# Three features of an input projection finished one pass earlier, and a planner's due times exchanged for fixed classes

## The chip, the cores and the metric

The kernel runs on one core of one Trainium2 chip, as one program. The metric is the device time of an execution in microseconds (us), as the median of several runs. Five engines work side by side, each with an instruction queue that it takes in order: TensorE (PE in the profile) multiplies, VectorE (DVE) and ScalarE (ACT) do elementwise work, GpSimd (POOL) has a few small steps here, and SyncE (SP) issues nearly all DMA transfers. Results of TensorE go to eight banks of a small memory (PSUM), from which VectorE or ScalarE have to clear them before the bank is used again.

## The reference

One encoder layer on x of 2048 tokens by 1024 features, in float32, cut to what matters:

```python
xn = rms_norm(x, mix_norm_g)
aq, ak, av, mq, mk, mv, mo, i, f, ga, gm = split(xn @ w_in)
A = chunk_band_attention(aq, ak, av, rel_bias)       # 8 heads of 64, own chunk of 64 and 8 before
mq, mk = silu(causal_conv(mq, mk))                    # width 4 along the tokens
M = sigmoid(mo) * rms_norm(mlstm_chunkwise(mq, mk, mv, i, f))   # 4 heads of 128
y = sigmoid(ga) * (A @ w_att_proj) + sigmoid(gm) * (M @ w_mlstm_proj)
x = x + y @ w_out
x = x + square(relu(rms_norm(x) @ w_up)) @ w_down
return rms_norm(x, final_norm_g)
```

## The kernel before

**Numbers and products.** Every float32 operand is split into a rounded high part (ScalarE, a cast) and the rest (VectorE, a subtraction), and each matrix product is three matmuls: high by high, high by low, low by high. A weight tile of 128 x 1024 is split by the two instructions at L582 and L584 (`split_now`); there are three slots for split weights (`wsp`) and four for raw ones (`wraw`). The large products use a scheme with seven products of half-sized sums in place of eight products of halves. The operands of the seven are numbered 0 to 6, and the four quarters of a result (a11, a12, a22, a21; the second place is the half of the tokens) come from sums of them: with p0 to p6 for the products and u2 = p0 + p3, they are a11 = p0 + p1, a12 = u2 + p2 + p4, a22 = u2 + p2 + p5 and a21 = u2 + p5 + p6. The sum v = u2 + p2 is used on the way to a22.

**Tokens.** There are four blocks of 512 tokens. The input projection of blocks 0 and 1 runs first ("quads", L712, all seven products of a feature in a row), and that of blocks 2 and 3 follows in `in_far`, at the same time as the attention and the recurrence (the "mixers") of blocks 0 and 1.

**The input projection of blocks 2 and 3.** `in_far` goes over the ten features of IN_ORDER (gm0, gm1, q, mq, vm, ga0, k, mk, ga1, mo) in three passes, since not all split operands fit at once: products (0, 3, 1), then (2, 4), then (5, 6), as BATCHES says. A product (`product`, L743, or L748 for vm) is one weight tile and 24 matmuls in two banks, for vm two weight tiles and 48. Pass one finishes a11 and parks u2 in device memory (`park_u2`). Pass two fetches u2 (`unpark`, L883), adds it to p2 and parks the sum v (`park_v`, L867), and finishes a12 (`finish_far`, L894). Pass three fetches v and u2 and finishes a22 and a21 (also L894). It goes through the features in the groups of PAIRS. What finishing is depends on the feature: for q and k a split and two stores, for the gates a tanh and a store, for mq and mk the convolution (`conv_far`, with L2208 three times and L2212 once for each result).

**Joint products.** Between the groups of pass three stand two joint products (`joint`, L1134, 168 matmuls each), which project the mixers' results of blocks 0 and 1. Their operands are loaded and split by `take_joint`, and their results, gated and added, become y. `take_y_late` loads y's parts k = 0 to 3 and splits them (L1355) into the operands of the output quads, which follow pass three at once (L712 again). For blocks 2 and 3, `project` does the projection inside the first down projection, at places that PROJ fixes.

**What sets the order.** The order of all instructions is written out when the program is built. A planner (`Flow`) runs the kernel's parts as threads against a model of the engines' times, and always takes the step that can start first. Among steps that could start at the same time, TensorE takes the one with the lower class (its spawn number, 0 to 5). On ScalarE, VectorE, GpSimd and SyncE the kernel before takes evictions marked "!" first and then the step with the earliest due time:

```python
if self.due is not None and e in ENGS:
    prio = -1e12 if prio < 0 else self.due.get((th.name, th.steps), 1e12)
key = (start, prio, th.n)
```

The due times come from a dry run of the whole program with empty tiles (`Blank`), whose log `dues` goes through backwards: a step is due when its earliest user has to begin, less its own duration and the latency between engines. In the dry run the classes decide. The framework underneath may still exchange neighbouring instructions within about 6 us on ScalarE and 10 us on VectorE of the planned time, and keeps the order beyond that.

**The start.** `norm_in` scales the first block's x (L1329, L1331) and squares it for the norm (L1338), and `split_first` splits the first weight tile in two halves (L565, L567). In the code the first square waits for both halves.

Of the kernel before, what the change touches and what calls it, by code (L numbers as in the profile page):

```python
# [28 lines left out]
P = 128  # L29
D = 1024  # L30
S = 2048
T = 512
# [22 lines left out]
PAIRS = ((0, 1), (2, 3), (4,), (5, 6), (7, 8), (9,))  # L55
# [7 lines left out]
JOINT = {(2, 2): 0, (2, 4): 1}  # L63
# [11 lines left out]
ENGS = ("act", "dve", "pool", "sp")  # L75
PEDUE = lambda prio: prio == 5
SPM = 0.0
TRIES = 1


class Event:
    def __init__(self):
        self.at = None
        self.by = ()


class Blank:


    def __getattr__(self, name):  # L90
        return self

    def __getitem__(self, at):
        return self

    def __call__(self, *a, **kw):
        return self

    def __iter__(self):
        raise TypeError("a blank has no parts")  # L100

    def tile(self, *a, **kw):
        return Blank()


class Pool:
    def __init__(self, items):
        self.free = [((0.0, "sp"), n, i, ()) for n, i in enumerate(items)]
        self.n = len(items)
# [15 lines left out]
class Thread:  # L125
    def __init__(self, gen, prio, n, at, name, by):
        self.gen, self.prio, self.n, self.at = gen, prio, n, at
        self.req = None
        self.name, self.kids, self.steps, self.by = name, 0, 0, list(by)


class Flow:
# [14 lines left out]
    def __init__(self, due=None):  # L147
        self.due = due
        self.log, self.cur = [], None
# [6 lines left out]
    def spawn(self, gen, prio=2):  # L156
        up = self.cur
        if up is None:
            th = Thread(gen, prio, self.count, self.now, f"{self.count}", ())
        else:  # L160
            th = Thread(gen, prio, self.count, self.now, f"{up.name}.{up.kids}", up.by)
            up.kids += 1
        self.count += 1
        self._step(th, None)

    def set(self, ev):
        ev.at = self.now
        ev.by = tuple(self.cur.by)

    def put(self, pool, *items, late=0.0):  # L170

        for i in items:
            by = tuple((x, y + late) for x, y in self.cur.by) if self.cur else ()
            pool.free.append(((self.now[0] + late, self.now[1]), pool.n, i, by))
# [4 lines left out]
    def _grant(self, th):  # L179
        kind, r = th.req[0], th.req  # L180
        if kind == "wait":
# [3 lines left out]
            th.by += [x for e in r[1] for x in e.by]  # L185
# [14 lines left out]
        th.by += [x for g in got for x in g[3]]  # L200
# [4 lines left out]
    def _step(self, th, value):  # L205
        keep, up = self.now, self.cur
        while True:
            self.now, self.cur = max(self.now, th.at), th
            try:
                th.req = th.gen.send(value)  # L210
            except StopIteration:
                self.now, self.cur = keep, up
                return
            self.cur = up
# [10 lines left out]
    def run(self):  # L225
        while self.ready or self.blocked:
# [15 lines left out]
            for th in self.ready:  # L242
                t, frm = th.at
                for e in th.req[0].split("|"):
# [12 lines left out]
                    if self.due is not None and e in ENGS:  # L257
                        prio = -1e12 if prio < 0 else self.due.get((th.name, th.steps), 1e12)
# [11 lines left out]
            at = th.name, th.steps  # L270
            self.log.append((at, e, start, end, th.prio, {x: y for x, y in sorted(th.by, key=lambda x: x[1])}))
            th.steps += 1
            th.by = [(at, 0.0)]
            th.at = self.now = (end, e)
            self._step(th, e)


def dues(log):
    late, of = {}, {x[0]: x[1:4] for x in log}
    due = {}  # L280
    for at, e, start, end, prio, by in reversed(log):
        end_by = late.get(at, 1e12) - (SPM if e == "sp" else 0.0)
        begin = end_by - (end - start)
        if e == "pe" and PEDUE(prio):
            begin = min(begin, start)
        due[at] = begin
        for x, wait in by.items():
            lat = Flow.LAT[of[x][0]].get(e, 0.0) + wait
            if e == "pe" and prio < 5:
                lat += Flow.FAR  # L290
            late[x] = min(late.get(x, 1e12), begin - lat)
    return due
# [20 lines left out]
class Layer:  # L313
    LATE, LANDED = 4000.0, 10000.0

    def __init__(self, nc, pool, psum, io, due=None):
# [2499 lines left out]
```

## Time and profile before

| what | value |
|---|---|
| time, median of 3 runs | 2733.04 us (2730.65 to 2734.66) |
| profiled execution, its own time | 2726.03 us |
| its span | 2724.2 us |
| granted clock of TensorE | 0.999 |
| instructions | 38141 |
| moved by DMA | 683.01 MB |

The profile is one execution, taken by the hardware profiler. Times are in us unless marked ns; PE is TensorE's matmuls, PEld its weight loads (which overlap the matmuls), and L12 is line 12 of the kernel. A group row gives line, engine, operation, out<-in by the program's tile names, shapes, the number of instructions, and then busy time, mean ns of one, and the idle time ahead of them with what ended it. A waits row names who waited for whom, the sum in us, how many times, and the longest. The chain that ended last follows the program back from its last instruction, at each step to what released it. Ends of matmuls are modelled, so one takes some 390 ns in these rows while the next starts 227 ns later.

### The profile page before, as it was taken

What the parts mean: (1) busy time and instruction counts of PE and PEld (TensorE: products, weight loads), DVE (VectorE), ACT (ScalarE), POOL (GpSimd) and SP (SyncE); (2) the same over time, 40 slices, a digit from 0 to 9 for tenths busy, and PEclk for the clock granted to TensorE, in tenths of its full rate; (3) what the DMA queues carried; (4) which work ended last, traced back from release to release, by engine and by line L of the source; (5) the groups of instructions that cost most, each with busy time, mean ns of one, the idle gap of its engine ahead of it and who ended that gap; (6) DMA issues with size and microseconds to landing.
All of it is one profiled execution on the core that took longest, in us unless ns stands there. A gap on an engine that the chain in (4) does not pass through costs nothing.

```text
span 2724.2 us, 38141 instructions
## 1 busy us (share of the span) xinstructions
PE 2706.6 (99%) x12784; PEld 2253.2 (83%) x12784; DVE 2109.8 (77%) x3750; ACT 1543.0 (57%) x2685; POOL 48.4 (2%) x79
## 2 busy tenths in 40 slices
PE   9999999999999999999999999999999999999998
PEld 8878888888888888888888888888888888888887
DVE  7878876888876899887768888889798665657675
ACT  6555456776753545566556766656345565554443
POOL 0000000000000000000000000000000000000000
PEclk9999999999999999999999999999999999999999
DMA  8777889878768889867768787766864454578863
GB/s 309 276 261 278 292 288 308 264 239 276 265 231 282 292 306 323 278 215 263 267 235 285 246 261 223 238 232 219 277 229 160 163 197 159 189 271 281 275 241 134
DMA packets 339304, 683.01 MB, mean 251 GB/s; under 512 B 37684, under 2 KB 66996, under 8 KB 339108
## 3 DMA queue, kind: packets, MB, share of 16 engines
q1 hardware_dynamic: 338388, 679.52, 73.2%
q8 instruction: 100, 1.64, 0.3%
q10 hardware_dynamic: 720, 1.06, 0.1%
q14 instruction: 96, 0.79, 0.1%
HBM read 461.41 MB, written 215.88 MB: 249 GB/s over the span
## 4 chain that ended last, share of the span: by engine, by line
PE 91%; DVE 3%; DMA 2%; issue 2%; ACT 1%; SPq 0%; POOL 0%; ACTq 0%; POOLq 0%; DVEq 0%
PE bank L712 40%; PE bank L743 9%; PE bank L644 8%; PE bank L645 8%; PE bank L643 8%; PE bank L1134 3%; PE bank L748 2%; PE bank L1612 2%; PE bank L1580 2%; PE bank L1505 2%; PE bank L970 1%; DVE wsp L584 1%; PE bank L1855 0%; PE bank L1840 0%; DMA ctx<-park 0%
## 5 line engine op out<-in xcount | busy, mean ns | idle before, releaser
L712 PE MATMUL bank<-r,wsp 128*128 128x512 f32 x4872 | 1110.3, 389 | 0.8 <-DVE wsp L584 0.7
L712 PEld LDWEIGHTS bank<-r,wsp 128*128 128x128 f32 x4872 | 913.2, 188 | 192.4 <-DVE wsp L584 1.2
L582 ACT CAST wsp<-wraw 128x1024 fp32r<-128x1024 f32 x437 | 459.1, 1051 | 495.3 <-PE bank L712 165.0
L584 DVE TENSOR_TENSOR wsp<-wraw,wsp 128x1024 fp32r<-128x1024 f32 x437 | 533.7, 1221 | 233.6 <-ACT wsp L582 228.6
L643 PE MATMUL bank<-r,wsp 128*128 128x512 f32 x960 | 379.3, 395 | 0.0
L645 PE MATMUL bank<-r,wsp 128*128 128x512 f32 x960 | 375.2, 391 | 0.0
L644 PE MATMUL bank<-r,wsp 128*128 128x512 f32 x960 | 375.2, 391 | 0.0
L743 PE MATMUL bank<-r,wsp 128*128 128x512 f32 x1512 | 368.1, 393 | 1.2 <-DVE ctx L894 1.0
L743 PEld LDWEIGHTS bank<-r,wsp 128*128 128x128 f32 x1512 | 279.0, 188 | 56.8 <-issue 1.0
L645 PEld LDWEIGHTS bank<-r,wsp 128*128 128x128 f32 x960 | 180.3, 188 | 38.4
L644 PEld LDWEIGHTS bank<-r,wsp 128*128 128x128 f32 x960 | 180.5, 188 | 33.6
L643 PEld LDWEIGHTS bank<-r,wsp 128*128 128x128 f32 x960 | 180.4, 188 | 33.4
L1353 DVE TENSOR_TENSOR r<-r 128x512 fp32r<-128x512 f32 x255 | 167.8, 683 | 19.1 <-ACT r L1348 18.3
L2041 DVE TENSOR_TENSOR ctx<-bank,ctx 128x512 f32<-128x512 f32 x174 | 118.9, 686 | 71.0 <-PE bank L712 69.7
L1348 ACT CAST r<-r 128x512 fp32r<-128x512 f32 x255 | 148.6, 616 | 32.0 <-DMA r<-u 28.6
L601 DVE TENSOR_TENSOR wraw<-wraw,wraw 128x1024 f32<-128x1024 f32 x112 | 136.3, 1218 | 3.3 <-DMA wsum<-wraw 2.3
L2033 ACT COPY ctx<-bank 128x512 f32<-128x512 f32 x174 | 101.1, 583 | 62.4 <-PE bank L712 46.5
L1593 ACT ACTIVATE sc<-sc,scs 128x640 f32<-128x640 f32 (+4 forms) x128 | 97.6, 763 | 68.6 <-DVE scs L1586 67.5
L2362 ACT ACTIVATE ctx<-ctx 128x512 f32<-128x512 f32 x96 | 60.5, 631 | 102.8 <-DVE ctx L2041 102.8
L1617 DVE TENSOR_TENSOR r<-bank,r 128x512 fp32r<-128x512 f32 (+1 forms) x168 | 95.7, 593 | 15.0 <-ACT r L1615 14.5
L1505 PE MATMUL bank<-r,r 128*128 128x512 f32 x336 | 94.8, 364 | 0.0
L1580 PE MATMUL bank<-r,r 128*128 128x256 f32 (+2 forms) x464 | 88.9, 312 | 1.6 <-DVE ctx L1896 0.7
(264 smaller groups left out, 3246.4 us busy)
## 6 DMA issues: line engine op xcount, KB each, us to landing
wraw<-in_wf SPq DMA_DIRECT2D x196, 512.0 KB, 4.8
r<-u SPq DMA_DIRECT2D x224, 256.0 KB, 4.1
wraw<-wsum SPq DMA_DIRECT2D x104, 512.0 KB, 4.9
u<-ctx SPq DMA_DIRECT2D x128, 256.0 KB, 2.2
ctx<-in_wf SPq DMA_DIRECT2D x104, 256.0 KB, 4.4
wsum<-ctx SPq DMA_DIRECT2D x104, 256.0 KB, 4.2
u<-tmp SPq DMA_DIRECT2D x96, 256.0 KB, 2.7
ctx<-park SPq DMA_DIRECT2D x66, 256.0 KB, 4.7
```

Of the source, the lines that this page charges most:

```text
L582: nc.scalar.copy(w[:, 0], raw)
L584: nc.vector.tensor_sub(w[:, 1], raw, w[:, 0].bitcast(F32))
L601: V.tensor_sub(dst, x, y)
L643: mm(ps, lh, rh, start=first, stop=False)
L644: mm(ps, lh, rl, start=False, stop=False)
L645: mm(ps, ll, rh, start=False, stop=last)
L712: mm(ps, wv[:, x, k, n], a[:, y], start=new and k == 0 and x == y == 0, stop=k == 3 and x == 1, skip_group_check=True)
L743: mm(ps, wv[:, x, k, n], a[:, y], start=start and x == y == 0, stop=stop and x == 1, skip_group_check=True)
L1348: self.nc.scalar.copy(dst[:, 0], src)
L1353: self.nc.vector.tensor_sub(dst[:, 1], src, dst[:, 0].bitcast(F32))
L1505: nc.tensor.matmul(bkv[:, :, c0:c0 + w], st, sl[:, :, o:o + w], start=n == 0, stop=n == total - 1)
L1580: nc.tensor.matmul(bk[:, :c1 - c0], q[:, y, i * P:(i + 1) * P], kf[:, f * P + c0:f * P + c1], start=y == 0, stop=y == 1)
```

## The change

The change has three parts.

1. *Three features in pass two.* Pass two does products 2 and 4 for the first seven features as before. For the last three (mk, ga1, mo) the new `in_both` does 2, 4, 5 and 6 in a row: v stays in a tile on the chip, a12 goes to a tile of its own, and all four quarters are done. Pass three has the other seven features alone. The joint products stand one group earlier in its list, ahead of groups 0 and 2 in place of 2 and 4, and `take_joint` starts with the last of the three features. The fetching of parked sums for pass three (`unpark`) starts behind them. The loader's list of weights follows.
2. *Classes in place of due times.* The dry run, `dues`, and all that recorded for them are removed. On all engines the step of the lower class goes first among those that could start together, then the older thread. In `take_y_late` the wait for the part before (k - 1) is dropped.
3. *The first square.* A dependency that is only an order on ScalarE's queue puts the first square behind the cast of the first weight tile's second half.

```diff
-PAIRS = ((0, 1), (2, 3), (4,), (5, 6), (7, 8), (9,))
+N_BOTH, J_FROM = 7, 9
+PAIRS = ((0, 1), (2, 3), (4,), (5, 6))
...
-JOINT = {(2, 2): 0, (2, 4): 1}
+JOINT = {(2, 0): 0, (2, 2): 1}
...
-                    if self.due is not None and e in ENGS:
-                        prio = -1e12 if prio < 0 else self.due.get((th.name, th.steps), 1e12)
                     key = (start, prio, th.n)
...
-def dues(log):
...
         for g, batch in enumerate(BATCHES):
-            for pair in PAIRS if g == 2 else [(i,) for i in range(len(IN_ORDER))]:
+            if g == 2:
+                yield from (part(Q_IN[name], m) for name in IN_ORDER[N_BOTH:] for m in (*BATCHES[1], *batch))
+            for pair in PAIRS if g == 2 else [(i,) for i in range(N_BOTH if g else len(IN_ORDER))]:
...
             if g == 2:
+                for i in range(N_BOTH, len(IN_ORDER)):
+                    if i == J_FROM:
+                        J = [self.operands() for _ in range(2)]
+                        fl.spawn(self.take_joint(0, J), 1)
+                    yield from self.in_both(i, A, aev, ring, got, gev, room)
+                ahead = pair(lambda: [None] * NT), pair(E4), Pool([0] * 6)
+                fl.spawn(self.unpark(g, kept, *ahead), 1)
+                got, gev, room = ahead
                 fl.put(self.rpool, *(yield "get", ring, 8))
-                J = [self.operands() for _ in range(2)]
                 slots = (yield "get", self.sc, 4), (yield "get", self.rpool, 6), [[Event(), Event()] for _ in range(6)]
-                fl.spawn(self.take_joint(0, J), 1)
...
+    def in_both(self, i, A, aev, ring, got, gev, room):
+
+        fl, name = self.fl, IN_ORDER[i]
+        finish, o = self.after_in(1, name), off(name)
+        release = ring if i == len(IN_ORDER) - 1 else None
+        v, one, two = [None] * 2, [], []
+        clear, done, vev = ([Event() for _ in range(2)] for _ in range(3))
+        yield from self.product(False, 2, A, aev, one, None, release)
+        for n in range(2):
+            fl.spawn(self.hold_v(n, got[i], gev[i], one[n], clear[n], v, vev[n], o), 1)
+        yield from self.product(False, 4, A, aev, one, clear, release)
+        for n in range(2):
+            fl.spawn(self.finish_12(finish, n, got[i], one[n], o), 1)
+        yield from self.product(False, 5, A, aev, two, None, None)
+        for n in range(2):
+            fl.spawn(self.finish_v(finish, n, two[n], done[n], v, vev[n], o), 1)
+        yield from self.product(False, 6, A, aev, two, done, None)
+        for n in range(2):
+            fl.spawn(self.finish_far(finish, n, "a21", 0, got[i], gev[i], two[n], None, o, room), 1)
+
+    def hold_v(self, n, got, gev, ps, clear, v, vev, o):
+        yield "wait", [gev[0][n]]
+        (v[n],) = yield "get", self.ctx, 1
+        yield "dve!", dve_ns(512)
+        self.nc.vector.tensor_add(v[n][:, o:o + 512], ps, got[0][n][:, o:o + 512])
+        self.fl.set(clear)
+        self.fl.set(vev)
+
+    def finish_12(self, finish, n, got, ps, o):
+        (t,) = yield "get", self.ctx, 1
+        yield "dve!", dve_ns(512)
+        self.nc.vector.tensor_add(t[:, o:o + 512], ps, got[0][n][:, o:o + 512])
+        self.fl.put(self.banks, ps)
+        yield from finish(n, "a12", t, None)
+
+    def finish_v(self, finish, n, ps, clear, v, vev, o):
+        yield "wait", [vev]
+        t = v[n]
+        yield "dve!", dve_ns(512)
+        self.nc.vector.tensor_add(t[:, o:o + 512], ps, t[:, o:o + 512])
+        self.fl.set(clear)
+        yield from finish(n, "a22", t, None)
...
     def take_y_late(self, s, k, O):
         if k > 1:
             yield "wait", [self.yp_ev[2 * s][k], self.yp_ev[2 * s][k + 4]]
-        if k > 0:
-            yield "wait", [O[1][m][k - 1] for m in range(7)]
         yield from self.take_y(s, k, *O)
...
-            nc.scalar.copy(w[:, 0, c], raw[:, c])
+            self.first_w = nc.scalar.copy(w[:, 0, c], raw[:, c])
...
         if b == k == 0:
             yield "wait", [self.wev[0], self.ev_w0]
         yield "act", act_ns(T)
-        nc.scalar.square(to[:, :T], x[:, :T])
+        done = nc.scalar.square(to[:, :T], x[:, :T])
+        if b == k == 0:
+            self.tc.add_manual_dep(done.ins, self.first_w.ins.name, mybir.DependencyInfo(
+                mybir.DependencyClass.NoSync, mybir.DependencyReason.DATA), reason="order")
```

More of the change, by code (lines that the diff above doesn't have):

```diff
@@ L83, in __init__ @@
         self.at = None
[L84 to L103, printed above, removed]
 class Pool:
     def __init__(self, items):
-        self.free = [((0.0, "sp"), n, i, ()) for n, i in enumerate(items)]
+        self.free = [((0.0, "sp"), n, i) for n, i in enumerate(items)]
         self.n = len(items)
@@ L145, with __init__ @@
                sp=dict())
[L147 to L149 removed]
+    def __init__(self):
         self.now = (0.0, "sp")
@@ L156, in spawn @@
     def spawn(self, gen, prio=2):
[L157 to L162, printed above, removed]
+        th = Thread(gen, prio, self.count, self.now)
         self.count += 1
@@ L167, in set @@
         ev.at = self.now
-        ev.by = tuple(self.cur.by)
     def put(self, pool, *items, late=0.0):
         for i in items:
-            by = tuple((x, y + late) for x, y in self.cur.by) if self.cur else ()
-            pool.free.append(((self.now[0] + late, self.now[1]), pool.n, i, by))
+            pool.free.append(((self.now[0] + late, self.now[1]), pool.n, i))
             pool.n += 1
@@ L205, in _step @@
     def _step(self, th, value):
-        keep, up = self.now, self.cur
+        keep = self.now
         while True:
-            self.now, self.cur = max(self.now, th.at), th
+            self.now = max(self.now, th.at)
             try:
@@ L269, in run @@
                 end += th.req[2]
[L270 to L273, printed above, removed]
             th.at = self.now = (end, e)
             self._step(th, e)
-def dues(log):
[L279 to L292, printed above, removed]
 def act_ns(n, ps=False, ap=0):
@@ L2788 @@
             past = {e: collections.deque() for e in ahead}
-            due = None
-            for _ in range(TRIES):
-                empty = Layer(Blank(), Blank(), Blank(), Blank(), due)
-                empty.build()
-                due = dues(empty.fl.log)
-            layer = Layer(nc, pool, psum, io, due)
+            layer = Layer(tc, pool, psum, io)
             def near(ins):
```

46 lines of the change are left out of this document (15 added, 31 removed).

## The prediction

> **What bounds the kernel now.** I read the page first, then busy time by stretch, then TensorE's waits, then the chain that ended last. From the page:
>
> ```profile
> span 2724.2 us, 38141 instructions
> PE 2706.6 (99%) x12784; PEld 2253.2 (83%) x12784; DVE 2109.8 (77%) x3750; ACT 1543.0 (57%) x2685; POOL 48.4 (2%) x79
> ...
> PE 91%; DVE 3%; DMA 2%; issue 2%; ACT 1%; SPq 0%; POOL 0%; ACTq 0%; POOLq 0%; DVEq 0%
> ...
> L712 PE MATMUL bank<-r,wsp 128*128 128x512 f32 x4872 | 1110.3, 389 | 0.8 <-DVE wsp L584 0.7
> L582 ACT CAST wsp<-wraw 128x1024 fp32r<-128x1024 f32 x437 | 459.1, 1051 | 495.3 <-PE bank L712 165.0
> L584 DVE TENSOR_TENSOR wsp<-wraw,wsp 128x1024 fp32r<-128x1024 f32 x437 | 533.7, 1221 | 233.6 <-ACT wsp L582 228.6
> ```
>
> TensorE is idle for 2724.2 - 2706.6 = 17.6 us, and 91% of the final chain lies on it. So nothing that leaves the matmuls alone can gain more than a part of 17.6 us, while it can lose any amount. The next fence is busy time by stretch (start:end, length, then each engine's busy us, granted clock, DMA share, GB/s). The stretches are the two in which the mixers (attention and recurrence) run beside dense products, the second input pass's end, the third pass, the quads behind it, an undisturbed stretch, and the tail.
>
> ```profile
> 454.00:750.00 296.00, 293.67 (x1616) 250.07 (x1615) 241.26 (x676) 212.61 (x481) 12.70 (x24) 1.00 0.82 263
> 855.00:921.00 66.00, 66.00 (x293) 53.52 (x292) 48.21 (x69) 34.34 (x51) 0.00 (x0) 1.00 0.85 291
> 921.00:1089.00 168.00, 165.77 (x728) 135.85 (x727) 158.05 (x242) 84.34 (x126) 0.00 (x0) 1.00 0.89 309
> 1089.00:1200.00 111.00, 110.26 (x485) 90.52 (x484) 100.51 (x135) 64.95 (x95) 0.00 (x0) 1.00 0.69 241
> 1200.00:1450.00 250.00, 250.00 (x1104) 207.02 (x1104) 183.59 (x244) 141.32 (x210) 0.11 (x1) 1.00 0.74 256
> 1450.00:1924.00 474.00, 471.83 (x2506) 401.21 (x2505) 405.37 (x991) 318.59 (x663) 16.63 (x31) 1.00 0.76 245
> 2640.00:2725.00 85.00, 76.06 (x352) 63.14 (x350) 48.97 (x73) 33.67 (x57) 4.18 (x5) 0.97 0.42 149
> ```
>
> The idle time splits up: 85.00 - 76.06 = 8.9 us is the tail, where the last rows are finished. The mixer stretches have 296 - 293.67 = 2.3 and 474 - 471.83 = 2.2, together 4.5 us. The third pass and the start of the quads have 2.2 + 0.7 = 3.0 us. The other 1.2 us lies in stretches not listed, the start mostly. What ended TensorE's waits there:
>
> ```profile
> PE bank L1612 <- ACT sc L1600: 1.4, 3, 1.0
> PE bank L1134 <- ACT ctx L2033: 1.3, 1, 1.3
> PE bank L743 <- DVE ctx L894: 1.0, 2, 0.5
> PE bank L1706 <- DVE g_lf L1704: 0.9, 1, 0.9
> PE bank L712 <- DVE wsp L584: 0.7, 1, 0.7
> ```
>
> L1134, L743 and L712 (1.3 + 1.0 + 0.7 = 3.0) are the third pass, the other two the mixers. VectorE is busy 158.05 of 168 us (94%) in the third pass and 48.21 of 66 (73%) just ahead of it. So the one place with a systematic cause is the third pass, where VectorE is nearly full.
>
> [...]
>
> **The change, part by part.** The multiplications stay the same: each of the three features (mk, ga1, mo) had two products in pass two and two in pass three and now has four in a row, each of 24 matmuls and one weight tile. A matmul's price comes from the chain, in this fence with the rows for the third pass (start, us, what):
>
> ```profile
> 982.97 28.44 PE bank L1134 x124
> ...
> 1040.80 7.00 DMA ctx<-park
> 1047.81 5.28 DMA ctx<-park
> ...
> 1090.79 1.29 DVE r L1355 x2
> ...
> 1093.21 1.15 DVE wsp L584
> ...
> 1094.40 349.70 PE bank L712 x1540
> ```
>
> 349.70 / 1540 = 0.227 us, so a product is 24 x 0.227 = 5.45 us and the matmul total moves by 0.
>
> *Transfers.* Per feature, the parked sum v (two tiles) is no longer stored, and in pass three neither v nor u2 (two tiles each) is loaded again.
>
> ```profile
> L883 SPq DMA_DIRECT2D ctx<-park x66: 319/407/1369, 708.3 to 1096.5; - x66
> L2286 SPq DMA_DIRECT2D park<-ctx x44: 319/320/1096, 470.6 to 882.4; - x44
> ```
>
> That takes 3 x 2 = 6 of the 44 stores and 3 x 4 = 12 of the 66 loads, 18 x 0.256 MB = 4.7 MB, and about 6 x 0.32 + 12 x 0.41 = 6.8 us of SP's issue time. It is worth 0 by itself: the chain passes through two such loads (7.00 and 5.28 us), but goes on through VectorE's queue before it reaches TensorE again. The reloads for the other features now start when the second pass is over, instead of one feature before, and have joint product 0 in front of them: 168 x 0.227 = 38 us of cover. If that were gone, the first group would wait for one load, 7 us.
>
> *VectorE's work moves.* The number of additions is unchanged (hold_v, finish_12, finish_v and one finish_far, against park_v and three finish_far). Prices from the groups of 1033 to 1100:
>
> ```profile
> L894 DVE TENSOR_TENSOR ctx<-bank,ctx 128x512 f32<-128x512 f32 x22 | 14.7, 680 | 0.0
> ...
> L2208 DVE SCALAR_TENSOR_TENSOR ctx<-ctx,cvw,ctx 128x512 f32<-128x512 f32 x12 | 8.8, 744 | 0.3 <-ACT ctx L2201 0.3
> ...
> L2212 DVE SCALAR_TENSOR_TENSOR ctx<-ctx,ctx 128x512 f32<-128x512 f32 x4 | 2.7, 684 | 0.0
> ```
>
> Four results a22 and a21 of mk cost 4 x (0.68 + 3 x 0.744 + 0.684) = 14.4 us, and the eight of ga1 and mo 8 x 0.68 = 5.4. These 20 us leave the end of the third pass for the place ahead of the joint products. Against that, both joint products and what prepares them come later by the six products now ahead less the four that were: 2 x 5.45 = 10.9 us. So the 94% falls by less than 20 / 168 = 12 points. [...]
>
> I don't take all of it, because the operands of the quads behind (take_y) start from joint product 1. It ended at 982.97 + 28.44 = 1011.4 and the quads began at 1094.4. Joint 1 ends 10.9 us later now and the quads begin no later, so this preparation has 10.9 us less. Its splits were the last work before TensorE already (L1355 at 1090.79). The wait that let its four parts go only one after another is dropped, which helps. Bounds: -3.0 (all three waits go) and +10.9 (all lost lead comes back). I take -1.3: the joint product's wait goes, the other two stay. The buffers that in_both holds (v, two of 16 context tiles) are within these bounds.
>
> *First square behind the first weights.* In time order at the start (ACT, then TensorE's wait):
>
> ```profile
> 4.26 0.61 ACT L1338 ACTIVATE sc<-ctx 128x512 f32<-128x512 f32 x1
> ...
> 4.78 0.60 ACT L565 CAST wsp<-wraw 128x512 fp32r<-128x512 f32 x1
> ...
> 6.18 0.62 ACT L565 CAST wsp<-wraw 128x512 fp32r<-128x512 f32 x1 [0.80 <-DMA wraw<-in_w]
> ...
> 9.57 1.03 ACT L582 CAST wsp<-wraw 128x1024 fp32r<-128x1024 f32 x1
> ...
> 11.91 0.50 PE L644 MATMUL bank<-wsp,r 128*128 128x512 f32 x1 [0.26 <-DVE wsp L584]
> ```
>
> The first cast came behind the square, so TensorE may start up to 4.78 - 4.26 = 0.5 us earlier. But the square's 0.61 us now falls behind the second cast, ahead of the cast at 9.57 for which TensorE waited at 11.91. Between -0.5 and +0.6, I take 0. The wait is an order on ACT's queue alone; the norm's scalings and casts queue behind it.
>
> *The order of the list.* Before, on ACT, VectorE, POOL and SP, the work that could start at the same time was ordered by the latest time it could start, found by a dry run of the whole program. Now it is ordered by class (evictions, then weight splits and loaded operands, then mixers and finishing, then the rest), and by age within one. In the dense stretches this hardly matters, since weights and evictions go first either way. It matters where the mixers run: a weight split there (1.05 us on ACT and 1.22 on VectorE, L582 and L584) may be far from due and still goes ahead of a mixer's step, on which a matmul already placed in TensorE's queue waits, with all dense matmuls behind it. The trace has no run under classes. Lower bound: the mixers' 4.5 us all go. Upper bound of this term: a wait, now at most about 1 us by the third number of those rows, takes a further pair of splits (1.05 + 1.22 = 2.3 us) and a little behind it, four times what it is, so 4 x 4.5 = 18, or +13.5. I take them tripled, +9.0: one split and its queue more for each wait, not always both.
>
> **Sum.** 0 - 1.3 + 0 + 9.0 = +7.7 us on the profiled execution's 2726.03 us, 2733.7. The three timed runs have a median of 2733.04, 7.0 above that execution, so 2740.7, say 2740. A measurement here tells about 0.2% (5.5 us) from no change.
>
> **Rivals.** *The order is as good as before.* The 8.9 us tail and the weights' supply don't hang on it, and TensorE's own order comes from the same rules in both. Then the third pass alone counts, -1.3 to -3.0: 2731. For it: VectorE has 14% to spare in 1450:1924 (405.37 of 474).
>
> *Faster: oldest first finishes the heads sooner.* Serving mixers by age, with no work held back to its latest start, would take away the mixers' 4.5 us along with the 3.0: -7.5, or 2725.5. It decides from 5.5 of these 7.5. Against it: nearly three quarters of it would have to go.
>
> *The last heads come late.* The fourth block's mixers must be done before its projection, which TensorE takes in its fixed order.
>
> ```profile
> 1921.25 0.69 DVE L1896 TENSOR_TENSOR ctx<-bank,tmp 128x512 f32<-128x512 f32 x1
> ...
> 1923.68 0.69 DVE L1353 TENSOR_TENSOR r<-ctx,r 128x512 fp32r<-128x512 f32 x1
> ...
> 2019.45 0.39 PE L712 MATMUL bank<-r,wsp 128*128 128x512 f32 x1
> ```
>
> The last operand was ready at 1923.68 + 0.69 = 1924.4. The projection (192 matmuls) and three quarters of the last down product (144) lie before 2019.45, so it begins at 2019.45 - 336 x 0.227 = 1943.2: 18.8 us to spare. If the mixers' 474 us grow by 10% (47.4), TensorE stands for 28.6 us: 2762. In the first half the mixers don't decide:
>
> ```profile
> 836.33 0.32 SPq L1541 DMA_DIRECT2D mix<-ctx  x1
> ...
> 910.57 1.32 PE L1134 MATMUL bank<-r,wsp 128*128 128x512 f32 x5
> ```
>
> There are 74 us between, and 10.9 more in the changed kernel.
>
> **How the numbers follow.** The forecast has 0.38, since the room to win is small and all of the order's uncertainty lies above; as good as before has 0.30; faster 0.20; late heads 0.12. Slower is 0.38 + 0.12 = 0.50. The range goes from the faster case's 2725 to the late heads' 2762, which leaves out half of the first and the upper part of the last. The forecast's own range is 2732 (order's term at 0) to 2752 (13.5 and some of the lost lead).
>
> **What would show it.** Right: TensorE's idle time in both mixer stretches grows to some 13 us, in short waits on ACT and VectorE at lines of the mixers, and the wait of the joint product is gone. Park stores number 38 and loads 54. VectorE is above 73% in the 66 us ahead of joint product 0, and below 94% in the third pass. Wrong: idle time there stays near 4.5 us; or one long wait at the fourth block's projection; or waits at the start of the quads (L712) beyond 1 us, which would be the lost lead.

## The result, and the profile after

The changed kernel takes 2737.02 us (median of 21 runs, 2733.50 to 2741.88), the kernel before 2731.07 us (median of 21 runs, 2726.61 to 2738.76). The ratio is 1.0023, with a 95% interval of 1.0017 to 1.0029: 6.0 us slower.

The profiled executions differ by more than that: 2738.3 against 2726.03 us, 12.3 us. The one of before lies 5.0 us below its median and the one of after 1.3 us above, so about half of what the two traces show against each other is what an ordinary pair of runs would show. From the page of the changed kernel (L653 was L712):

```profile
span 2736.5 us, 38107 instructions
PE 2713.6 (99%) x12784; PEld 2254.9 (82%) x12784; DVE 2109.3 (77%) x3747; ACT 1545.8 (56%) x2688; POOL 48.9 (2%) x79
...
PE 82%; DVE 6%; issue 5%; DMA 4%; ACT 2%; POOL 0%; SPq 0%; POOLq 0%; DVEq 0%; ACTq 0%
...
L653 PE MATMUL bank<-r,wsp 128*128 128x512 f32 x4872 | 1111.7, 390 | 3.3 <-ACT r L1334 1.2
```

The matmuls are as many as before. TensorE's idle time went from 17.6 us to 2736.5 - 2713.6 = 22.9, and its share of the chain that ended last from 91% to 82%, with VectorE, ScalarE and DMA in its place: there are more waits, and they are longer. Its busy time rose too, by 7.0 us from 2706.6, for the same matmuls. So idle time doesn't hold the whole loss: some matmuls run at a lower granted clock (0.57 and 0.51 in two windows of the last section), and a wait shows only from the modelled end of the matmul before it, about 0.39 - 0.227 = 0.16 us after the next one could have started. Below, what a stretch "loses" is TensorE's idle time in it. Next stands busy time by stretch in the changed kernel, with the columns of the prediction's table, and behind it the one stretch of before that was not shown there.

```profile
454.00:750.00 296.00, 290.53 (x1575) 244.10 (x1574) 238.48 (x659) 203.24 (x461) 12.79 (x23) 1.00 0.83 263
750.00:855.00 105.00, 103.17 (x508) 86.02 (x507) 73.22 (x143) 49.83 (x102) 3.39 (x5) 0.98 0.78 261
855.00:921.00 66.00, 66.00 (x293) 54.66 (x292) 53.01 (x80) 30.67 (x42) 0.00 (x0) 1.00 0.66 227
921.00:1089.00 168.00, 166.02 (x726) 135.53 (x725) 145.13 (x217) 84.35 (x127) 0.00 (x0) 0.99 0.88 296
1089.00:1200.00 111.00, 109.15 (x476) 88.55 (x475) 102.96 (x144) 63.99 (x96) 0.00 (x0) 1.00 0.74 253
1450.00:1924.00 474.00, 473.22 (x2498) 402.85 (x2497) 401.10 (x980) 320.45 (x654) 18.70 (x30) 1.00 0.79 248
```
```profile
750.00:855.00 105.00, 105.00 (x510) 87.31 (x509) 72.28 (x129) 45.96 (x91) 2.79 (x4) 1.00 0.74 248
```

The first mixers (454 to 855) lose 5.5 + 1.8 = 7.3 us, 2.3 before. The second mixers lose 0.8, 2.2 before. The third pass and the start of the quads (921 to 1200) lose 1.98 + 1.85 = 3.8, 3.0 before. VectorE's load ahead of the third pass rose to 53.01 of 66 us (80%, from 73%) and in it fell to 145.13 of 168 (86%, from 94%). The granted clock is below 1 in two stretches (0.98 from 750 to 855, 0.99 from 921 to 1089), which the section on the hardware takes up.

Counting matmuls gives the loss whole. From 454 to 855 TensorE starts 1575 + 508 of them against 1616 + 510 before: 43 fewer, worth about 43 x 0.227 = 9.8 us. More exactly, take the matmul that starts at some time in the trace of before, and the start of the one with the same number in the trace of after. The second is later by 1.6 us at 454, 11.2 at 855, 11.3 at 921, 13.8 at 1200, 14.2 at 1450 and 13.0 at 1924. So the first mixers add 9.6 us, nearly twice what their idle time shows, the third pass and the start of the quads 2.6, and the second mixers take back 1.3.

TensorE's three largest waits over the whole run, and below them ScalarE's waits for the mask that GpSimd prepares for a recurrence head (L1774; its user L1804 is the head's first exponential), of which the kernel before has none:

```profile
PE bank L1487 <- DVE r L1599: 2.7, 2, 1.8
PE bank L1594 <- ACT sc L1582: 2.1, 2, 1.9
PE bank L689 <- ACT r L1336: 2.0, 1, 2.0
```
```profile
ACT ctx L1804 <- POOL ctx L1774: 9.8, 5, 3.9
```

Such a wait is followed here on three engines, in the timeline of the changed kernel (start, us, what, and the idle time before it with what ended it): ScalarE, then GpSimd, then two rows of TensorE.

```profile
753.77 0.58 ACT L1498 COPY tmp<-bank 64x512 f32<-64x512 f32 x1 [0.47 <-PE bank L1487]
758.21 1.28 ACT L1804 ACTIVATE ctx<-ctx,g_u 128x128 f32<-128x128 f32 x4 [3.85 <-POOL ctx L1774]
759.39 1.03 ACT L523 CAST wsp<-wraw 128x1024 fp32r<-128x1024 f32 x1
...
761.27 0.37 ACT L1597 CAST r<-bank 128x256 fp32r<-128x256 f32 x1
```
```profile
757.54 0.64 POOL L1774 TENSOR_SCALAR_AFFINE_SELECT ctx<-ctx 128x512 f32<-128x512 f32 x1 [17.99 <-DMA ctx<-mrow]
```
```profile
755.56 0.38 PE L1594 MATMUL bank<-const,sc 128*128 128x128 f32 x2
...
762.48 0.51 PE L1487 MATMUL bank<-r,r 128*128 128x256 f32 x2 [1.83 <-DVE r L1599]
```

ScalarE stands for 3.85 us at an exponential whose mask row has not come in. From 758.21 on it has no gap, so the casts behind it in its queue (759.39, 761.27) are later for it, and so is the matmul that needs the second of them through VectorE: TensorE stands for 1.83 us. The input of that second cast, two small matmuls of L1594, had been there since about 756. The first cast is a weight split of the kind that the prediction feared: with 24 matmuls to a weight tile, counted over the trace, its tile is first used at 776.37, 17 us later, and it still goes ahead of the mixer's cast. Up to 1.03 of the 1.83 us are its share; the mask's is the larger.

### The profile page after: what moved, and what is told of

The parts are those of the page before. It is cut to its first block, busy times and chain, and to the rows that moved or that the text cites. A ratio compares the mean times of both kernels' runs of the same rounds, so it can differ in the third digit from the quotient of the medians.

```text
span 2736.5 us, 38107 instructions
## 1 busy us (share of the span) xinstructions
PE 2713.6 (99%) x12784; PEld 2254.9 (82%) x12784; DVE 2109.3 (77%) x3747; ACT 1545.8 (56%) x2688; POOL 48.9 (2%) x79
## 4 chain that ended last, share of the span: by engine, by line
PE 82%; DVE 6%; issue 5%; DMA 4%; ACT 2%; POOL 0%; SPq 0%; POOLq 0%; DVEq 0%; ACTq 0%
PE bank L653 36%; PE bank L684 9%; PE bank L585 8%; PE bank L584 8%; PE bank L586 8%; PE bank L1119 2%; PE bank L689 2%; PE bank L1562 2%; PE bank L1487 2%; PE bank L1594 2%; PE bank L955 1%; DVE wsp L525 1%; DMA ctx<-mrow 1%; ACT wsp L523 1%; PE bank L1645 1%
## 5 line engine op out<-in xcount | busy, mean ns | idle before, releaser
L653 PE MATMUL bank<-r,wsp 128*128 128x512 f32 x4872 | 1111.7, 390 | 3.3 <-ACT r L1334 1.2
L653 PEld LDWEIGHTS bank<-r,wsp 128*128 128x128 f32 x4872 | 912.6, 188 | 197.0 <-ACT r L1334 1.9
L1599 DVE TENSOR_TENSOR r<-bank,r 128x512 fp32r<-128x512 f32 (+1 forms) x168 | 95.9, 594 | 13.9 <-ACT r L1597 13.1
L1597 ACT CAST r<-bank 128x512 fp32r<-128x512 f32 (+1 forms) x168 | 81.1, 515 | 31.8 <-PE bank L1594 29.7
```

What stands on the lines that cost most here:

```text
L653: mm(ps, wv[:, x, k, n], a[:, y], start=new and k == 0 and x == y == 0, stop=k == 3 and x == 1, skip_group_check=True)
```

## The experiments

Each kernel was timed in five rounds beside the kernel before on the same chip. "Wait kept" means the wait for the part before (k - 1) in `take_y_late`. All of them compute the whole layer.

**The classes alone.** The kernel before without its dry run.

```diff
-TRIES = 1
+TRIES = 0
```

> The kernel before with one line changed: no dry run, so no due times, and classes alone give the order. The three features, the joint products, the wait in take_y_late and the first square stay as before. Theory (the order by classes costs the time, through waits of TensorE in the mixer stretches): slower by 6 to 10 us, TensorE's idle time in 454:750 at 5 us or more (2.3 before), the third pass worse than before as its relief is missing. Rival (the three features cost it, by the shorter lead of the output operands): within 2 us of before.

2748.99 us, ratio 1.0063 [1.0050, 1.0075]: by the ratio 17 us slower, far more than the whole change. Windows and waits:

```profile
1089.00:1200.00 111.00, 105.15 (x449) 84.26 (x448) 95.72 (x131) 61.45 (x89) 0.00 (x0) 0.98 0.69 229
```
```profile
PE bank L712 <- ACT r L1350: 4.5, 1, 4.5
...
ACT ctx L1822 <- POOL ctx L1792: 8.7, 4, 3.9
```

5.9 us are lost from 1089 to 1200, 0.7 before: the operands of the first quads come late. The first mixers lose 8.9 us, with the same waits for masks. So the rest of the change takes back two thirds of what the classes cost.

**The three features alone, wait kept.** The kernel before with part 1 of the change: `in_both`, the shorter PAIRS, JOINT one group earlier, the due times left in.

```diff
+N_BOTH, J_FROM = 7, 9
+PAIRS = ((0, 1), (2, 3), (4,), (5, 6))
+JOINT = {(2, 0): 0, (2, 2): 1}
...
+                    yield from self.in_both(i, A, aev, ring, got, gev, room)
```

> The kernel before with the three features finished in pass two and the joint products moved, still ordered by due times, with the wait in take_y_late and the first square as before. Theory: faster by about 1.3 us, between 3 us faster and no difference; the joint product's wait is gone. Rival: slower by 3 to 6 us, with waits of 1 to 2 us of TensorE at vm in the third pass or at the first output quad, as in the changed kernel.

2737.43 us, 1.0023 [1.0014, 1.0032]. In the profile the loss stands where the prediction put its upper bound, at the start of the quads (L715 here):

```profile
1089.00:1200.00 111.00, 106.04 (x448) 84.58 (x447) 98.29 (x134) 60.56 (x89) 0.00 (x0) 0.97 0.67 226
```
```profile
PE bank L715 <- ACT r L1397: 3.0, 3, 1.4
```

TensorE is idle for 4.96 us there, 0.74 before, waiting for the splits of the quads' operands. By themselves, with the wait kept, the three features are a loss.

**The first square alone.**

```diff
-        nc.scalar.square(to[:, :T], x[:, :T])
+        done = nc.scalar.square(to[:, :T], x[:, :T])
+        if b == k == 0:
+            self.tc.add_manual_dep(done.ins, self.first_w.ins.name, ...)
```

> The kernel before with the first square put behind the first weights' casts and nothing else. Both theories: between 0.6 us slower and 0.5 us faster, which can't be told from no change. Should it move by 2 us or more, a small edit of the list reshuffles enough around it to matter, and differences of 2 us between lists are no evidence on a mechanism.

2732.94 us, 1.0008 [0.9999, 1.0018]: not to be told from none. The profile has a wait of 2.66 us at 219 us that the profile of before doesn't have:

```profile
221.98 3.01 PE L712 MATMUL bank<-r,wsp 128*128 128x512 f32 x12 [2.66 <-DVE ctx L2044]
```

VectorE, which TensorE waits for here, has itself stood for 4.25 us at a small copy into a buffer that a store (`wsum<-ctx`) still had to read. It is hardly of the edit's making. All five kernels of the experiments that follow due times on all four engines have it in their profiles, with 1.96 to 3.23 us of TensorE and 3.6 to 4.3 us of VectorE; in the profile of before VectorE stands there for 1.97 us and TensorE not at all. In the kernel with the dropped wait alone even the order of TensorE's matmuls is that of before up to 1080 us. So the profile of before, 5.0 us under its median, was probably lucky at this place; a second profile of it, which would show that, was not taken. The kernels with classes on all engines don't have the wait: their traces gain some 3 to 6 us here against those five. Single waits of 2 to 3 us are no evidence below.

**Classes and three features, wait kept.** The second experiment's kernel with TRIES = 0.

> Classes and the three features in pass two, without the first square's order and with the wait in take_y_late kept. Theory: slower than before by 5 to 9 us, like the changed kernel, and about 1 to 3 us faster than classes alone. Rival: 6 us slower than before, and 4 us or more slower than classes alone.

2743.65 us, 1.0050 [1.0037, 1.0064]. The classes add 6 us to the second experiment, not the 17 that they add to the kernel before.

**The changed kernel with the due times back.**

```diff
+                    if self.due is not None and e in ENGS:
+                        prio = -1e12 if prio < 0 else self.due.get((th.name, th.steps), 1e12)
...
+                due = dues(empty.fl.log)
```

> The changed kernel with the due times put back: the three features in pass two, the first square's order, the dropped wait in take_y_late, but the order by due times as before. If the classes cost the changed kernel its time and the dropped wait gives the output operands their lead back: within 3 us of the kernel before, with no wait over 1 us at the first output quad. If the three features cost it whatever the order: slower than before by 5 us or more, as they were with the wait kept.

2731.32 us, 1.0002 [0.9994, 1.0011]: level with the kernel before. So the classes cost the changed kernel 2737.02 - 2731.32 = 5.7 us, and the three features, the dropped wait and the square together nothing that shows. Its windows:

```profile
454.00:750.00 296.00, 294.20 (x1617) 250.74 (x1616) 238.73 (x673) 210.35 (x475) 12.58 (x24) 1.00 0.84 263
...
1089.00:1200.00 111.00, 109.76 (x484) 90.25 (x483) 104.51 (x143) 62.73 (x92) 0.00 (x0) 1.00 0.73 248
```

The first mixers lose 1.8 us instead of 7.3, and no exponential waits for a mask. Counted by matmuls, the trace wins 0.8 us there against before, where the changed kernel adds 9.6. So the 5.7 us are a balance. Between the two traces, which lie some 7 us apart, the classes cost 10.4 us in the first mixers and 3.3 from 921 to 1200, and win 2.3 ahead of the mixers (at the store), 2.0 in the second mixers and 2.4 behind them.

**The changed kernel with the wait put back.**

```diff
+        if k > 0:
+            yield "wait", [O[1][m][k - 1] for m in range(7)]
```

> The changed kernel with the wait of part k for part k - 1 put back in take_y_late, nothing else. If the dropped wait is what makes up for the 10.9 us of lead that the moved joint products take from the output operands: 5 to 8 us slower than the changed kernel (11 to 14 us above the kernel before), all of it in waits of TensorE between 1085 and 1130 at the start of the output quads. If it is the first square's order that made the difference between the changed kernel and classes with the three features: no slower than the changed kernel.

2743.04 us, 1.0043 [1.0031, 1.0055]: 6.0 us above the changed kernel. They stand at the first quads (L653), where 7.13 us are lost instead of 1.85:

```profile
1089.00:1200.00 111.00, 103.87 (x445) 82.24 (x444) 96.81 (x132) 60.24 (x89) 0.00 (x0) 1.00 0.69 234
```
```profile
PE bank L653 <- ACT r L1338: 4.5, 4, 2.7
```

The dropped wait pays for the lead that the three features take away.

**The exponentials held back.** The changed kernel, with the planner told that the load of a head's mask row lands in 6000 ns instead of 2000 (in the trace it takes 3.7 to 5.4 us, median 4.6).

```diff
-        yield "sp", 800, 2000
+        yield "sp", 800, 6000
```

> The changed kernel in which the planner takes 6 us in place of 2 us for the landing of the row that a recurrence head's mask is made of (7.5 us from issue to mask in the changed kernel's trace), nothing else; the instructions are the same, in another order. If TensorE's waits in the first mixer stretch come from ScalarE standing at the head's first exponentials until GpSimd has made the mask (9.8 us in 5 waits): these waits fall below 2 us, TensorE's idle time in 454:855 falls from 7.3 us by 3 us or more, the half clock at 763 is gone, and the kernel is 3 to 6 us faster than the changed one. If they come from weight splits that go ahead of mixer steps: no change within 2 us.

2741.78 us, 1.0037 [1.0025, 1.0049]: slower than the changed kernel, against what was expected. In the first mixers it did what it should:

```profile
454.00:750.00 296.00, 292.00 (x1566) 245.24 (x1565) 237.60 (x651) 204.00 (x453) 11.13 (x21) 1.00 0.85 268
```
```profile
PE bank L653 <- ACT wsp L523: 2.7, 1, 2.7
...
ACT ctx L1804 <- POOL ctx L1774: 3.5, 2, 2.4
```

The waits for masks fell from 9.8 to 3.5 us, and TensorE's idle time from 454 to 855 from 7.3 to 4.0, all of it ahead of 750. Counted by matmuls, the first mixers still add 7.2 of the 9.6 us. And the new list has waits elsewhere, the longest 2.7 us at 1086 for a weight split. So by these traces the late masks cost some 2.4 us in the list of the changed kernel, a quarter of what its first mixers add; taking them away doesn't by itself give a better list.

**Weight splits behind the mixers.** The changed kernel with the prediction's mechanism undone: the loads and splits of the large products' weights get class 1.5 instead of 0.

```diff
-            fl.spawn(self.split_w(...), 0)
+            fl.spawn(self.split_w(...), 0 if kind == "plain" else 1.5)
```

> The changed kernel with the loading and splitting of the weight tiles of the input passes and the down projection moved from the first class to one behind the mixers (1.5), nothing else. If weight splits far from due cost TensorE its waits in the mixer stretches, as the prediction had it: idle time in 454:855 falls from 7.3 us by 3 us or more and the kernel is faster by as much, unless weights come late elsewhere. If ScalarE standing for a mask costs them: the waits at the masks stay, and the kernel is the same or slower.

2747.13 us, 1.0059 [1.0047, 1.0070]: 10 us slower than the changed kernel.

```profile
PE bank L689 <- DVE wsp L525: 6.7, 1, 6.7
...
ACT ctx L1804 <- POOL ctx L1774: 5.5, 4, 3.7
```

One weight comes 6.7 us late (at 1056), and the first mixers lose 9.65 us, more than the 7.3 of which a part should have been won back; none of TensorE's waits there is for a weight. TensorE's granted clock in this trace was 0.99 from 454 to 750 and 0.98 from 921 to 1089, where the trace of before has 1.00. Weight splits that go first have a share in single waits, as in the one followed above, but they aren't what makes the first mixers slow in the main: with the splits put behind, these are slower still.

**Without the square's order.** The due times, the three features and the dropped wait, the square where it was.

> The changed kernel with the due times back and the first square where it was (so three features and the dropped wait alone, in due order). Theory: the parts besides the order are worth little together, and the square's own +2 in the earlier run was only another list: 2729 to 2733, within 2 us of the run with the square. Rival: the square itself costs time at the start: 1 to 2 us below that run, with TensorE's first matmul earlier by 0.5. Rival 2: the square wins 0.5 at the start: 0.5 above it.

2730.48 us, 0.9998 [0.9989, 1.0006]: level with the kernel before, and with the fifth experiment. The square is worth nothing that shows.

**Due times on ScalarE alone.** The fifth experiment's kernel, in which only some engines follow the due times.

```diff
-ENGS = ("act", "dve", "pool", "sp")
+ENGS = ("act",)
```

> The changed kernel with due times on ScalarE alone; VectorE, GpSimd and SyncE keep the classes. Theory (the loss comes from ScalarE's order, where the heads' first exponentials stand for a mask that is late): 2730 to 2734, waits of ScalarE for the mask below 1 us together (9.8 in the changed kernel), idle time of TensorE in 750:855 below 0.5. Rival (VectorE's or SyncE's order): 2735 to 2740, as the changed kernel.

2736.14 us, 1.0017 [1.0008, 1.0026]. This is a miss: most of the loss stays, the first mixers lose 6.1 us, and ScalarE still waits for masks for 4.0 us (2.7 of it in this stretch). Windows and TensorE's longest waits there:

```profile
454.00:750.00 296.00, 290.12 (x1568) 243.20 (x1567) 241.89 (x669) 193.22 (x445) 14.02 (x24) 1.00 0.83 263
```
```profile
PE bank L1553 <- DVE r L1665: 2.1, 4, 0.8
PE bank L746 <- DVE r L1665: 1.1, 2, 0.6
```

**Due times on the other three.** The mirror image.

```diff
-ENGS = ("act", "dve", "pool", "sp")
+ENGS = ("dve", "pool", "sp")
```

> The mirror image: due times on VectorE, GpSimd and SyncE, classes on ScalarE alone. Theory (ScalarE's order): 2735 to 2740 like the changed kernel, with 5 to 10 us of ScalarE waiting for masks and waits of TensorE of 1.5 us and more beside them. Rival (the others' order): 2730 to 2733.

2737.67 us, 1.0025 [1.0014, 1.0035], as that theory expected, but the theory fell with its twin: each half of the due times leaves the loss in place. The first mixers lose 6.4 us, and the mask waits are 4.8 us.

**The dropped wait alone.** The kernel before, with due times, without features and square.

```diff
-        if k > 0:
-            yield "wait", [O[1][m][k - 1] for m in range(7)]
```

> The kernel before with nothing but the wait for the part before (k - 1) dropped in take_y_late. If dropping it is a gain by itself: the idle time of TensorE in 1089:1200 falls from 0.7 to near 0 and the time by at most that, 2730 to 2731. If it only repays the lead that the three features take: within 2 us of before, either sign, from another list. Rival: the four parts together crowd VectorE ahead of the quads: 3 us and more above before, in waits behind 1089.

2738.50 us, 1.0028 [1.0018, 1.0037]: in size the rival holds. The third pass and the quads' start lose 6.4 us instead of 3.0, but nearly half of it (3.13 us) ahead of 1089, where the rival had it all behind. That VectorE is crowded isn't shown: it is busy for 154.99 of 168 us in the third pass, less than before (158.05). The longest wait, first on TensorE, then on ScalarE:

```profile
1071.40 1.08 PE L743 MATMUL bank<-r,wsp 128*128 128x512 f32 x2 [2.77 <-ACT wsp L582]
```
```profile
1069.79 0.63 ACT L2148 ACTIVATE tmp<-ctx 128x512 fp32r<-128x512 f32 x1 [2.92 <-DVE ctx L894]
1070.32 1.03 ACT L582 CAST wsp<-wraw 128x1024 fp32r<-128x1024 f32 x1
```

ScalarE stands for 2.92 us at a step that needs a sum of VectorE's, and the cast that TensorE waits for is next in its queue. It is the same kind of wait as at the masks, this time in a list by due times.

All kernels together. The idle times are those of TensorE in the profiled executions (length of the windows less PE's busy time), and the last column is what the first mixers add in the trace, counted by matmuls of the same number against before:

| kernel | order | features in pass two | k - 1 wait | ratio | idle 454:855 | idle 921:1200 | added 454:855 |
|---|---|---|---|---|---|---|---|
| before | due | no | kept | 1 | 2.3 | 3.0 | 0 |
| square alone | due | no | kept | 1.0008 | 1.8 | 3.1 | -0.4 |
| dropped wait alone | due | no | dropped | 1.0028 | 2.8 | 6.4 | 0.5 |
| features, wait kept | due | yes | kept | 1.0023 | 4.1 | 6.4 | 2.0 |
| all but the classes | due | yes | dropped | 1.0002 | 1.8 | 2.4 | -0.8 |
| the same without square | due | yes | dropped | 0.9998 | 2.6 | 2.6 | 0.2 |
| classes alone | classes | no | kept | 1.0063 | 8.9 | 10.1 | 9.6 |
| classes, features | classes | yes | kept | 1.0050 | 8.2 | 7.2 | 9.0 |
| the same, with square | classes | yes | kept | 1.0043 | 8.0 | 9.0 | 8.9 |
| the changed kernel | classes | yes | dropped | 1.0023 | 7.3 | 3.8 | 9.6 |
| exponentials held back | classes | yes | dropped | 1.0037 | 4.0 | 4.8 | 7.2 |
| splits behind the mixers | classes | yes | dropped | 1.0059 | 9.7 | 8.2 | 13.1 |
| due on ScalarE alone | mixed | yes | dropped | 1.0017 | 6.1 | 6.2 | 7.1 |
| due on the other three | mixed | yes | dropped | 1.0025 | 6.4 | 4.4 | 5.7 |

Two things are shown by it. With due times on all four engines, the first mixers lose 1.8 to 4.1 us and add at most 2.0; with classes on some or all of them they lose 6.1 to 9.7, or 4.0 where the exponentials were held back, and add 5.7 to 13.1. And the features and the dropped wait are each a loss of 6 to 8 us alone and nothing together. One delays the quads' operands and the other lets them start early, into a third pass where VectorE is busy for 154.99 of 168 us without the features and for 146.16 with them. That the room on VectorE is the reason is only argued, and the kernel before, with 158.05 us there and few waits, speaks against it; no run changed it alone. None of the kernels is faster than the one before.

What stays open is why half of the due times does no better than none. A due time is worked out as if every engine kept to it; that this is why they fail singly wasn't tested.

## Why the prediction was right, and where not

The forecast was 2740, the result 2737.0, inside the forecast's own range; it came out slower by 0.23%, at the edge of what was called telling.

*What bounds it.* Right in that the matmuls are the same and that the loss lies in waits and what comes with them. But the prediction took TensorE's idle time for the whole of that, and here it shows only 5.3 of the 12.3 us between the two traces; the rest counts as busy.

*Transfers and matmuls at nothing.* Right: 12784 matmuls, and the park traffic as counted, in the page's rows of DMA issues (tiles, times, KB each, median us to landing).

```profile
ctx<-park SPq DMA_DIRECT2D x54, 256.0 KB, 5.9
...
park<-ctx SPq DMA_DIRECT2D x38, 256.0 KB, 4.3
```

*VectorE's work, -1.3.* The direction was right: 80% ahead of the third pass, 86% in it, the wait of the joint product gone. The sum wasn't. With due times the stretch 921 to 1200 gains 0.4 to 0.6 us of idle time, under classes it loses 0.9 (2.6 counted by matmuls). The upper bound, 10.9 us of lost lead, was the real danger: with the wait kept, 6 us of it come back in both orders. The term came out near its value only because of the dropped wait, which the prediction called a help and gave no price. It costs 7 us without the features and wins 6 with them.

*The first square, 0.* Right within what can be measured, by two pairs of kernels.

*The order, +9.0.* The size came near, the account behind it failed in the main. By the medians the classes cost 5.7 us; counted by matmuls against before, both mixer stretches together add 9.6 - 1.3 = 8.3, and the classes win some of it back elsewhere. But the added time lies in the first alone. In the second the waits went from 2.2 to 0.8 us, where the forecast had the loss in both, some 13 us of idle time against 7.3 + 0.8 = 8.1. The prediction had a weight split go ahead of a mixer's step while far from due. The trace has this, with up to 1.03 us in the wait that was followed. But putting the splits behind made things worse by 10 us, and what weighs more in that wait is an engine with its queue in order standing at a step whose input isn't there, ScalarE for 3.85 us at the exponentials for masks. That too is one such wait among several, not the cause of all: without most of the late masks the first mixers still add 7.2 us, and with due times on one half of the engines or the other, the masks' waits halve and other short waits make up the loss. So that the number fits is in part luck. The upper bound of this term, +13.5, was too low for the classes by themselves, which cost 17 us, since it took the mixers alone and left out the quads' start.

*The sum and its base.* The prediction's base, the median 7.0 us above the profiled execution, comes out as 2731.07 - 2726.03 = 5.0 over 21 runs. This explains 2.0 of the 3.7 us between its 2740.7 and the result; the other 1.7 is the sum, +7.7 against +6.0. That the sum lies so near is luck too: the two traces, to which its terms belong, differ by 12.3, and neither the wait at the store nor the price of the dropped wait was in it.

*The rivals.* "The order is as good" gave 2731, and that is what the changed kernel takes with the due times back, 2731.3. "Oldest first is faster" had a point in the second mixers (-1.4 us) and lost it threefold in the first. "The last heads come late" came nearer than the time shows. The last operand in the changed kernel, and the first matmul behind the projection and the down product:

```profile
1950.31 0.68 DVE L1339 TENSOR_TENSOR r<-ctx,r 128x512 fp32r<-128x512 f32 x1
```
```profile
2031.92 4.24 PE L653 MATMUL bank<-r,wsp 128*128 128x512 f32 x18
```

By the prediction's own count the projection begins at 2031.92 - 336 x 0.227 = 1955.6, and the operand was ready at 1951.0: 4.6 us to spare of 18.8. The classes do serve the heads later; they use up slack there and no time.

## What to carry to other kernels

Where TensorE has only 1% to lose, look in the trace for the engine that stands in its queue with an operand of TensorE's behind it: 3.85 us of idle time on ScalarE, which is busy for 56% of the span and looks far from a bound, cost 1.83 us on TensorE. Parts of a change that shift the same work in time (here an earlier feature and a dropped wait) have to be priced as a pair, for alone each may have the other sign. Idle time can show half of a loss (5.0 of 9.6 us in the first mixers), so compare the starts of the same matmul in both traces as well. And two traces may differ by twice what the kernels do, so set each against its median before the difference is explained.

## What the hardware showed that was not expected

After two waits of TensorE of under 2 us its clock was at half. In the changed kernel they are the wait of 1.83 us that ended at 762.48 (its row stands above) and one of 1.98 us that ended at 1066.37 (busy time by stretch; the column behind the brackets of POOL is the granted clock):

```profile
757.00:763.00 6.00, 4.17 (x24) 3.42 (x23) 2.54 (x8) 4.77 (x11) 0.64 (x1) 1.00 1.04 396
763.00:767.00 4.00, 4.00 (x13) 3.27 (x13) 2.94 (x9) 3.95 (x10) 0.00 (x0) 0.57 1.00 366
767.00:771.00 4.00, 4.00 (x25) 3.46 (x24) 3.64 (x8) 4.00 (x9) 0.00 (x0) 1.00 0.51 163
```
```profile
1067.00:1070.50 3.50, 3.50 (x10) 2.73 (x9) 3.50 (x6) 0.23 (x1) 0.00 (x0) 0.51 0.96 332
```

The trace's clock records put the half clock at 763.32 and at 1067.10, 0.84 and 0.73 us after those waits, for 3.41 us each time, so that 13 matmuls, some of them small, fall into 4 us where 4 / 0.227 = 17.6 large ones would. By an estimate each such window costs 3.41 / 2 = 1.7 us, which shows as busy time and not as a wait: with it the wait of 1.83 us costs 3.5. The 18 large matmuls from 1066.37 on fit the estimate: they take 5.94 us, where 18 x 0.227 + 0.16 = 4.25 would do at the usual pace. The two starts are 303.78 us apart, 89.0 times the length of 3.413 us that the records give each of them. The trace's third half clock starts at 2732.81, behind TensorE's last matmul and 1665.71 us after the second, 488.0 times that length. So in this trace the starts lie whole multiples of it apart.

What it takes for a half clock isn't settled by these traces. In the same trace none followed the wait of 1.92 us that ended at 505.65: the granted clock is 1.00 from 454 to 750, where 3.41 us at half would make it 0.99. Nor did one follow the wait of 2.21 us that ended at 551.51 in the kernel with due times on the other three (1.00 from 454 to 750), or the wait of 2.66 us that ended at 221.98 in the kernel with the square alone (1.00 from 0 to 250). So the length of a wait alone didn't decide it in these runs, and what did was not shown. The prediction counted waits at their length and left this out: by the estimate above, 3.4 of the 12.3 us between the two traces are these two windows.
